# Running the narrow and the wide form of an expert side by side, weight tile by weight tile

## The chip, the cores and the metric

The kernel runs on one NeuronCore of a Trainium2 chip. The metric is the device time of one execution in microseconds. TensorE (PE in the profile; PEld is its weight load) multiplies, VectorE (DVE) and ScalarE (ACT) work elementwise, GpSimd (POOL) does small copies, and SyncE (SP) issues the DMAs that bring the weights from HBM.

## The reference

One encoder layer, 256 tokens of width 2048, float32. A first half (modulated norm, input projection, attention, spatial gating, output projection, norm) is not touched by the change. The second half is a mixture of 32 experts: each token goes to two experts of one group of eight.

```python
    xs = xf[row_tok].reshape(n_blocks, EXPERT_BLOCK, d)      # rows sorted by expert

    def expert_block(args):
        xb, e = args
        hb = jax.nn.silu(xb @ w_gate[e]) * (xb @ w_up[e])    # 2048 -> 512
        return hb @ w_down[e]                                # 512 -> 2048
...
    out = jax.ops.segment_sum(ys * row_w[:, None], row_tok, num_segments=n)
```

So 512 rows (256 tokens, two experts each) are spread over 32 experts as the router has it, and every expert with at least one row needs its 12 MB of float32 weights. The result goes into a last residual and norm.

## The kernel before, in words

**First half** (to about 770 us). Modulation vectors, projections and attention stream their weights through a ring of SBUF tiles. None of it is changed.

**The experts.** The rows of all experts lie side by side, sorted by expert, as columns of `xs`. On the chip the experts are sorted by their number of rows, and the order of work is a list of 32 *places* (`place`, lines 140 to 144): place 0 is expert 0, and of the rest those with the most rows stand at the places 2, 6, 10, 14, 18 and 22 (`WIDE`, line 40). A group is four places, so each of the first six groups has a wide place third. Places 24 to 31 run only if they have rows; in this data 28 places run.

**The weight ring.** A place needs twelve tiles of 1 MB: eight with gate and up weights (`gu`, 256 rows of the contraction each) and four with down weights (`dn`). They go through one ring of 14 tiles (lines 655 and 901: `ring`, `ringw`, `ringm`, `ringl`). SP issues the loads in order (`chunk`, line 92, called by `load_place`); a load into a tile waits until TensorE's last read of the tile's former weights.

**The narrow form** (`narrow`) takes the first 32 rows of the expert. As each gate-up tile arrives, TensorE multiplies it in pieces of 128 columns at four places of the array (shape 128x32, four products at a time, line 955). Then `act`: silu on ACT (934), product on DVE (935), transpose on TensorE (938), copy on ACT (939). The down product (961) again goes tile by tile into `pdn`. DVE multiplies `pdn` by the gate and puts it into 32 rows of `y4` (966). After four places `add_four` spreads `y4` over the tokens by a product with slot weights `sl` and adds it into the residual `xa` (1088, 1089), with squares on ACT (1081) for the last norm.

**The wide form** (`wide`) takes rows 33 to 96 of an expert (`xw`, 64 columns, copied by POOL ahead of the place). In `at_place` a wide place loads its row count into registers of PE, ACT and DVE, runs `narrow` up to its last down product, and then, inside `tc.If(v > 32)` on these three engines, the whole of `wide`: a product that selects the expert's slots and weights (`sel_rows`, 1003), two slot-weight tiles on DVE (917, 918), gate-up over all eight tiles once more (978, shape 128x64, two at a time), the same activation chain, the down product (985), two multiplications on DVE (990), and eight products and additions into `xa` (`add_rows`, 926 and 928). Only then come the narrow form's four multiplications into `y4`.

**The order.** TensorE, ACT and DVE run in program order (`manual_schedule`), as do SP and POOL. `group` runs three places, then makes the group's slot weights (`sel_rows` with a small copy `selt` on DVE, line 1001, then a product and `slot_rows`), then the fourth place, then `add_four`.

Of the kernel before, what the change touches and what calls it, by code (L numbers as in the profile page):

```python
# [11 lines left out]
AF = mybir.ActivationFunctionType  # L12
# [4 lines left out]
KT = 16  # L17
NT = 2
T = 256
# [24 lines left out]
def trunk_kernel(ctx, tc, x, c_t, w_ada1, w_ada2, b_ada, b_adac, w_in, sgu_wt, sgu_b, sgu_ln, w_pr, w_o, w_r, b_r,  # L44
                 w_gu, w_down, ln1_c, ln1_g, ln1_b, ln2_g, ln2_b, out):
    nc = tc.nc
# [19 lines left out]
    def k1(name, dt=F32):  # L66
        return wk.tile([128, 256], dt, name=name, tag="k1", bufs=5)
# [4 lines left out]
    def pb(name):  # L72
        return ps.tile([128, 512], F32, name=name, tag="pb", bufs=4)
# [844 lines left out]
        V.tensor_mul(sl, sl, psl[:, 256:])  # L918
        return sl

    def add_rows(sl, y):

        for n in range(NT):
            for j in range(4):
                po = pb("po")
                TE.matmul(po, sl(j)[:, n * 128:(n + 1) * 128], y(j), start=True, stop=True)
                s = xa[n][:, 512 * j:512 * (j + 1)]
                V.tensor_add(s, s, po)

    def act(p, w, own=None):  # L930

        sg, hb, hbT = [own[:, 256 * i:256 * (i + 1)] for i in range(3)] if own is not None else \
            (k1("sg"), k1("hb"), k1("hbT"))
        S.activation(sg[:, :w], p[:, :w], AF.Silu)  # L934
        V.tensor_mul(hb[:, :w], sg[:, :w], p[:, w:2 * w])  # L935
        pt = pa("ptr")
        for i in range(w // 128):
            TE.transpose(pt[:, i * 128:(i + 1) * 128], hb[:, i * 128:(i + 1) * 128], ident)
        S.copy(hbT[:, :w], pt[:, :w])
        return hbT  # L940

    def gate_up(gu, c, k):
        return gu[c].rearrange("p (k a f) -> p k a f", k=2, a=2)[:, k]

    def narrow(gu, dn, rows, el, order=range(8), before_c=None, between=None):

        pn = pa("pgun")
        for i, c in enumerate(order):
            if before_c:
                before_c(i)  # L950
            for k in range(2):
                kt = 2 * c + k
                w = gate_up(gu, c, k)
                for j in range(4):
                    TE.matmul(pn[32 * j:32 * j + 32, :256].rearrange("p (a f) -> p a f", a=2), rows[:, kt],  # L955
                              w[:, :, 128 * j:128 * (j + 1)], start=i + k == 0, stop=i + k == 8)
        hn = act(pn, 128)
        pdn = pa("pdn")
        for j in range(4):
            for n in range(4):  # L960
                TE.matmul(pdn[32 * n:32 * n + 32, :], hn[:, 32 * j:32 * j + 32], dn[j][:, 512 * n:512 * (n + 1)],  # L961
                          start=j == 0, stop=j == 3)
        if between:
            between()
        for n in range(4):
            V.tensor_mul(y4[32 * el:32 * el + 32, 512 * n:512 * (n + 1)], pdn[32 * n:32 * n + 32, :],  # L966
                         gate2[0][32 * n:32 * n + 32, :])

    def wide(gu, dn, rows, col, own=None):


        psl = rows()
        sl = [slot_rows(psl, col + h, own and own[0][:, 1024 + 256 * h:1280 + 256 * h]) for h in range(2)]
        pw = pa("pguw")
        for kt in range(KT):
            w = gate_up(gu, kt // 2, kt % 2)
            for j in range(2):
                TE.matmul(pw[64 * j:64 * j + 64, :].rearrange("p (a f) -> p a f", a=2), xw[:, kt],
                          w[:, :, 256 * j:256 * (j + 1)], start=kt == 0, stop=kt == KT - 1)
        hw = act(pw, 256, own and own[0])  # L980
        pdw = [pb(f"pdw{b}") for b in range(2)]
        for j in range(4):
            l = hw[:, (j % 2) * 128 + 64 * (j // 2):(j % 2) * 128 + 64 * (j // 2) + 64]
            for n in range(4):
                TE.matmul(pdw[n // 2][64 * (n % 2):64 * (n % 2) + 64, :], l, dn[j][:, 512 * n:512 * (n + 1)],
                          start=j == 0, stop=j == 3)
        ys = []
        for b in range(2):
            y = own[1][:, 512 * b:512 * (b + 1)] if own else k2("yw")
            V.tensor_mul(y, pdw[b], g64[:, b])  # L990
            ys.append(y)
        add_rows(lambda j: sl[j % 2], lambda j: ys[j // 2])

    def sel_rows(c0, c1, rep):
        psl = pb("psl")
        lhs = ident[:32, c0:c1]
        if rep == 128:
            lhs = lhs.to_broadcast([32, 128])
        else:
            t = k1("selt")[:32, :128]  # L1000
            V.tensor_copy(t.rearrange("p (e s) -> p e s", s=rep), lhs[:, :, None].to_broadcast([32, c1 - c0, rep]))
            lhs = t
        TE.matmul(psl, lhs, rwT[:32], start=True, stop=True)
        return psl

# [21 lines left out]
    def leftovers():  # L1027

        r, own = ring, (y4, misc[:, 1024:])
        with tc.For_i(0, NE, 1) as i:  # L1030
            va = nc.values_load(cnt[:1, bass.ds(i + AS, 1)], min_val=0, max_val=2)
            with tc.If(va > 0):
                es = nc.sync.value_load(cnt[:1, bass.ds(i + ES, 1)], min_val=0, max_val=NE - 1)
                for t, src in zip(r, sources(bass.ds(es, 1))):
                    nc.sync.dma_start(t, src.rearrange("a p c -> (a p) c"))
                ev = nc.vector.value_load(cnt[:1, bass.ds(i + ES, 1)], min_val=0, max_val=NE - 1)
                rc = wk.tile([128, 2, NT], F32, name="rc", tag="rc")
                V.tensor_copy(rc, rw[:, :, :, bass.ds(ev, 1)].rearrange("p a n e -> p a (n e)"))

                def rows():  # L1040
                    psl = pb("pslf")
                    for n in range(NT):
                        for a in range(2):
                            TE.transpose(psl[:, a * 256 + n * 128:a * 256 + (n + 1) * 128],
                                         rc[:, a, n:n + 1].to_broadcast([128, 128]), ident)
                    return psl

                def rest(j):
                    off = 32 + 64 * j
                    f = nc.vector.value_load(cnt[:1, bass.ds(i + FS, 1)], min_val=0, max_val=512 - off - 1)  # L1050
                    V.tensor_copy(xw, xs[:, :, bass.ds(f + off, 64)])
                    wide(r[:8], r[8:], rows, 1 + 2 * j, own=own)
# [17 lines left out]
    narrow(*first_weights, xs[:, :, :32], 0, order=range(7, -1, -1), before_c=rows0)  # L1070
    gate2_halves()


# [18 lines left out]
    ENG = (E.PE, E.Activation, E.DVE)  # L1092

    def at_place(i, sl=None):
# [3 lines left out]
        if i not in WIDE:  # L1098
            narrow(gu, dn, xnb[i % 2], i % 4)
            return  # L1100
        f = nc.gpsimd.value_load(cnt[:1, WS + i // 4:WS + i // 4 + 1], min_val=32, max_val=512)
        P.tensor_copy(xw, xs[:, :, bass.ds(f, 64)])
        v = nc.values_load(cnt[:1, CS + i:CS + i + 1], engines=ENG, min_val=0, max_val=T)

        def more_rows():
            with tc.If(v > 32):
                wide(gu, dn, lambda: sel_rows(i, i + 1, 128), 1)

        narrow(gu, dn, xnb[i % 2], i % 4, between=more_rows)

    def group(q):
        for i in range(max(1, 4 * q), 4 * q + 3):
            at_place(i)
        sl = slot_rows(sel_rows(4 * q, 4 * q + 4, 32), 0)
        if q == 6:
            tc.mark_branch_hint_location("rare", hint="LikelyTaken", engines=ENG)
        at_place(4 * q + 3)
        add_four(sl)

    l2 = []  # L1120

# [101 lines left out]
```

## Time and profile before

| | |
|---|---|
| three timed runs | 1681.76 us median (1676.31 to 1685.01) |
| the profiled execution's own time | 1673.7 us |
| its span | 1672.0 us |
| TensorE busy, mean granted clock | 1373.1 us (82%), 0.891 |
| DVE, ACT, POOL busy | 797.8, 386.5, 56.6 us |
| HBM read | 572.38 MB, mean 345 GB/s |

The span is the stretch of the profiled execution that has instructions, 1.7 us shorter than its time. The page gives the busy time of each engine and slices the span in forty; the other views give single waits, instructions in order of time, and busy times by stretch. A TensorE that is busy is not at its peak: its products overlap, and the records run on past the end of streaming. Because the page's chain of waits goes back only to the last branch that all engines share (1655.8 us here), the experts' stretch has to be read from the other views.

### The profile page before, as it was taken

The numbers are of one execution on the slowest core, as the hardware profiler recorded it, in microseconds if no ns is written. First come the engines' busy times: TensorE is split into PE (matmuls) and PEld (weight loads), VectorE is DVE, ScalarE is ACT, GpSimd is POOL, SyncE is SP. The second block draws the span as 40 slices with busy tenths as digits, with TensorE's granted clock in tenths as the row PEclk, the third lists the DMA queues.
The fourth block names the chain that finished last, engine by engine and source line by source line (L and its number), as shares of the span: only waits on it lengthen the run. The fifth ranks groups of instructions, "written<-read, shape, count | busy, mean of one in ns | idle before, by whom it ended". The sixth has DMA issues, their size and how long they took to land. (4 is left out here: it accounts for less than half of the span.)

```text
span 1672.0 us, 24699 instructions
## 1 busy us (share of the span) xinstructions
PE 1373.1 (82%) x10150; PEld 862.1 (52%) x10151; DVE 797.8 (48%) x1099; ACT 386.5 (23%) x519; POOL 56.6 (3%) x76
## 2 busy tenths in 40 slices
PE   4999999999999989967788688688688678767664
PEld 3878989989999987744223123123223223222121
DVE  6777879788877767875123013104104104112104
ACT  2533244663333332333101001001001000101002
POOL 0000000001000100000000000000000000000000
PEclk8999999999999998987889789779879889878677
DMA  8978787478998888884988998988998998999994
GB/s 327 363 294 309 308 299 278 173 257 334 336 340 321 308 331 301 325 327 153 417 363 354 421 393 360 421 351 362 421 397 365 421 398 360 420 418 422 421 421 194
DMA packets 80353, 576.17 MB, mean 345 GB/s; under 512 B 9448, under 2 KB 9448, under 8 KB 10600
## 3 DMA queue, kind: packets, MB, share of 16 engines
q1 hardware_dynamic: 78624, 569.41, 85.7%
q10 hardware_dynamic: 1608, 5.10, 0.8%
q8 instruction: 82, 1.34, 0.3%
q14 instruction: 39, 0.32, 0.0%
HBM read 572.38 MB, written 2.10 MB: 344 GB/s over the span
## 5 line engine op out<-in xcount | busy, mean ns | idle before, releaser
L195 DVE TENSOR_TENSOR wl<-ring,wh 128x2048 fp32r<-128x2048 f32 x95 | 217.6, 2291 | 22.7 <-ACT wh L194 22.6
L194 ACT CAST wh<-ring 128x2048 fp32r<-128x2048 f32 x95 | 180.9, 1906 | 152.1 <-DMA ring<-in_w_in 56.5
L935 DVE TENSOR_TENSOR hb<-sg,pgun 128x128 f32<-128x128 f32 x28 | 8.1, 288 | 336.2 <-ACT sg L934 336.2
L342 DVE SCALAR_TENSOR_TENSOR acc<-ring,csg,acc 128x1024 f32<-128x1024 f32 x120 | 153.6, 1280 | 5.9 <-DMA ring<-in_w_ada 4.3
L966 DVE TENSOR_TENSOR y<-pdn,comp 32x512 f32<-32x512 f32 x112 | 76.9, 687 | 159.2 <-PE pdn L961 157.6
L934 ACT ACTIVATE sg<-pgun 128x128 f32<-128x128 f32 x28 | 7.8, 278 | 576.6 <-PE pgun L955 576.6
L203 PE MATMUL a<-hT,wh 128*128 128x256 f32 x384 | 109.7, 287 | 0.0
L204 PE MATMUL a<-hT,wh 128*128 128x256 f32 x384 | 108.2, 283 | 0.0
L205 PE MATMUL a<-hT,wl 128*128 128x256 f32 x384 | 107.8, 284 | 0.0
L955 PE MATMUL pgun<-ringm,misc 128*32 128x256 f32 x1024 | 85.2, 479 | 26.3 <-DMA ringm<-in_w_gu 26.3
L955 PE MATMUL pgun<-ring,misc 128*32 128x256 f32 x992 | 77.2, 454 | 30.1 <-DMA ring<-in_w_gu 30.1
L955 PE MATMUL pgun<-ringw,misc 128*32 128x256 f32 x960 | 76.0, 461 | 30.1 <-DMA ringw<-in_w_gu 30.0
L205 PE MATMUL gb<-hT,wl 128*128 128x256 f32 x256 | 74.2, 290 | 7.5 <-DVE wl L195 7.5
L203 PEld LDWEIGHTS a<-hT,wh 128*128 128x128 f32 x384 | 73.6, 192 | 6.3 <-issue 3.6
L955 PEld LDWEIGHTS pgun<-ringm,misc 128*32 128x32 f32 x1024 | 34.3, 130 | 80.2 <-DMA ringm<-in_w_gu 46.9
L205 PEld LDWEIGHTS a<-hT,wl 128*128 128x128 f32 x384 | 73.1, 192 | 2.1 <-DVE qT L296 0.8
L205 PE MATMUL ga<-hT,wl 128*128 128x256 f32 x256 | 73.0, 285 | 1.1 <-DVE wl L195 1.1
L204 PEld LDWEIGHTS a<-hT,wh 128*128 128x128 f32 x384 | 73.6, 192 | 0.4 <-issue 0.2
L203 PE MATMUL gb<-hT,wh 128*128 128x256 f32 x256 | 73.5, 287 | 0.0
L204 PE MATMUL gb<-hT,wh 128*128 128x256 f32 x256 | 73.1, 286 | 0.0
L203 PE MATMUL ga<-hT,wh 128*128 128x256 f32 x256 | 72.8, 285 | 0.0
L204 PE MATMUL ga<-hT,wh 128*128 128x256 f32 x256 | 72.4, 283 | 0.0
(404 smaller groups left out, 2589.8 us busy)
## 6 DMA issues: line engine op xcount, KB each, us to landing
ring<-in_w_ada SPq DMA_DIRECT2D x87, 1024.0 KB, 6.1
ring<-in_w_gu SPq DMA_DIRECT2D x66, 1024.0 KB, 18.4
ringw<-in_w_gu SPq DMA_DIRECT2D x64, 1024.0 KB, 16.1
ringm<-in_w_gu SPq DMA_DIRECT2D x64, 1024.0 KB, 19.1
ring<-in_w_in SPq DMA_DIRECT2D x63, 1024.0 KB, 6.4
ringm<-in_w_down SPq DMA_DIRECT2D x32, 1024.0 KB, 18.9
ringw<-in_w_down SPq DMA_DIRECT2D x32, 1024.0 KB, 19.7
ring<-in_w_down SPq DMA_DIRECT2D x32, 1024.0 KB, 19.7
```

The source lines that it names most:

```text
L194: S.copy(wh, w)
L195: V.tensor_sub(wl, w, wh)
L203: TE.matmul(acc, lh, rh, start=first, stop=False)
L204: TE.matmul(acc, lh, rl, start=False, stop=False)
L205: TE.matmul(acc, ll, rh, start=False, stop=last)
L342: V.scalar_tensor_tensor(acc, ws, c, acc, op0=ALU.mult, op1=ALU.add)
L934: S.activation(sg[:, :w], p[:, :w], AF.Silu)
L935: V.tensor_mul(hb[:, :w], sg[:, :w], p[:, w:2 * w])
L955: TE.matmul(pn[32 * j:32 * j + 32, :256].rearrange("p (a f) -> p a f", a=2), rows[:, kt], w[:, :, 128 * j:128 * (j + 1)], start=i + k == 0 ...
L966: V.tensor_mul(y4[32 * el:32 * el + 32, 512 * n:512 * (n + 1)], pdn[32 * n:32 * n + 32, :], gate2[0][32 * n:32 * n + 32, :])
```

## The change

`narrow`, `wide`, `act`, `gate_up` and `add_rows` become one function `expert`, which takes the narrow form, the wide form, or both. At the six wide places it runs both, always: the row count is no longer loaded on PE, ACT and DVE, and the `If` is gone. For each gate-up tile TensorE issues the narrow products and then the wide ones, and for each down tile the same. The two activation chains are issued as silu and product of the narrow form, the same of the wide form, the selection product, then transpose and copy of each. The two slot-weight tiles come after that, and the adds of the wide form and the four multiplications into `y4` at the end, in this order. In `group` the product that selects the group's slots moves from between the third and fourth place into the fourth place, between gate-up and transpose (its copy `selt` stays ahead of the place), and `slot_rows` for it moves behind the fourth place.

```diff
+    def expert(gu, dn, narrow=None, wide=None, order=range(8), before_c=None, in_chain=None, own=None):
...
+        pn = narrow and pa("pgun")
+        pw = wide and pa("pguw")
         for i, c in enumerate(order):
...
+            for k in range(2):
+                if narrow:
+                    gate_up(pn, 4, narrow[0], c, k, i)
+            for k in range(2):
+                if wide:
+                    gate_up(pw, 2, xw, c, k, i)
+        hn = narrow and hidden(pn, 128)
+        hw = wide and hidden(pw, 256)
+        extra = in_chain and in_chain()
+        if wide:
+            psl = wide[0]()
+        hn = narrow and turned(*hn, 128)
+        hw = wide and turned(*hw, 256)
+        if wide:
+            sl = [slot_rows(psl, wide[1] + h, own and own[0][:, 1024 + 256 * h:1280 + 256 * h]) for h in range(2)]
+        pdn = narrow and pa("pdn")
+        pdw = wide and [pb(f"pdw{b}") for b in range(2)]
         for j in range(4):
             for n in range(4):
+                d = dn[j][:, 512 * n:512 * (n + 1)]
+                if narrow:
+                    TE.matmul(pdn[32 * n:32 * n + 32, :], hn[:, 32 * j:32 * j + 32], d, start=j == 0, stop=j == 3)
             for n in range(4):
...
+                if wide:
...
+                    TE.matmul(pdw[n // 2][64 * (n % 2):64 * (n % 2) + 64, :], l, d, start=j == 0, stop=j == 3)
...
-        v = nc.values_load(cnt[:1, CS + i:CS + i + 1], engines=ENG, min_val=0, max_val=T)
-
-        def more_rows():
-            with tc.If(v > 32):
-                wide(gu, dn, lambda: sel_rows(i, i + 1, 128), 1)
-
-        narrow(gu, dn, xnb[i % 2], i % 4, between=more_rows)
+            wide = lambda: sel_rows(ident[:32, i:i + 1].to_broadcast([32, 128])), 1
+        return expert(gu, dn, (xnb[i % 2], i % 4), wide, in_chain=in_chain)
 
     def group(q):
         for i in range(max(1, 4 * q), 4 * q + 3):
             at_place(i)
-        sl = slot_rows(sel_rows(4 * q, 4 * q + 4, 32), 0)
...
-        at_place(4 * q + 3)
-        add_four(sl)
+        t = k1("selt")[:32, :128]
+        V.tensor_copy(t.rearrange("p (e s) -> p e s", s=32), ident[:32, 4 * q:4 * q + 4, None].to_broadcast([32, 4, 32]))
+        psl = at_place(4 * q + 3, lambda: sel_rows(t))
+        add_four(slot_rows(psl, 0))
```

## Rows read from the trace of the kernel before

**Rows 1.** The page: the span, and of the 40 slices of the span (41.8 us each) the granted TensorE clock in tenths and what the DMA engines moved.

```profile
span 1672.0 us, 24699 instructions
...
PEclk8999999999999998987889789779879889878677
...
GB/s 327 363 294 309 308 299 278 173 257 334 336 340 321 308 331 301 325 327 153 417 363 354 421 393 360 421 351 362 421 397 365 421 398 360 420 418 422 421 421 194
```

**Rows 2.** Busy time by stretch from the second expert on: per row the stretch, its length, then busy us and instruction count of PE, PEld, DVE, ACT and POOL, the granted TensorE clock as a share of 2.4 GHz, the DMA share and the GB/s moved. The middle stretch holds all the wide branches that were taken.

```profile
800.00:840.00 40.00, 29.94 (x330) 10.63 (x322) 6.27 (x12) 2.61 (x7) 1.23 (x2) 0.82 1.01 422
840.00:1470.00 630.00, 490.12 (x3785) 169.79 (x3785) 137.75 (x269) 44.53 (x128) 17.02 (x24) 0.86 0.94 387
1470.00:1620.00 150.00, 101.29 (x809) 30.53 (x805) 23.01 (x47) 9.23 (x26) 2.47 (x4) 0.72 1.01 420
```

**Rows 3.** The same view around the first wide place, 840 to 890 us, same columns.

```profile
840.00:842.50 2.50, 1.08 (x12) 0.16 (x8) 0.00 (x0) 0.00 (x0) 0.00 (x0) 0.86 1.01 419
842.50:852.50 10.00, 10.00 (x34) 2.92 (x32) 1.72 (x4) 0.00 (x0) 0.00 (x0) 0.69 0.48 172
852.50:880.00 27.50, 22.85 (x90) 7.82 (x86) 9.64 (x15) 0.76 (x2) 0.00 (x0) 0.99 1.01 422
880.00:887.50 7.50, 6.79 (x62) 2.88 (x66) 1.52 (x4) 0.00 (x0) 0.00 (x0) 0.59 0.24 79
887.50:890.00 2.50, 2.50 (x52) 1.40 (x48) 0.00 (x0) 0.00 (x0) 0.00 (x0) 1.00 1.05 334
```

**Rows 4.** Waits of the SP queue, which issues the weight loads: who waited at which line for whom, us in total, times, longest.

```profile
SPq L92 <- PE pgun L955: 132.4, 69, 14.2
SPq L92 <- PE pguw L978: 124.8, 40, 19.9
```

**Rows 5.** The SP queue's timeline over the first of these gaps: start, us from the first to the last issue, queue, line, tile, count of transfers issued (1024 KB each).

```profile
848.74 2.09 SPq L92 DMA_DIRECT2D ringm<-in_w_gu  x2
852.21 0.33 SPq L92 DMA_DIRECT2D ring<-in_w_gu  x1
```

**Rows 6.** Timeline around the first wide place: start, us, engine, line, operation, tile, shapes, count; in brackets the idle time ahead and what ended it. An fp32 product shows as two records. Narrow gate-up paced by the DMA; selection product; wide gate-up (16, 32 and 16 records); silu; wide down; the first add into the residual rows; the four narrow evictions.

```profile
826.54 1.85 PE L955 MATMUL pgun<-ring,misc 128*32 128x256 f32 x16 [0.63 <-DMA ring<-in_w_gu]
843.01 2.07 PE L1003 MATMUL psl<-rwT,ident 32*128 32x512 f32 x2
845.01 5.44 PE L978 MATMUL pguw<-ringm,xw 128*64 128x512 f32 x16
850.28 7.03 PE L978 MATMUL pguw<-ring,xw 128*64 128x512 f32 x32
857.15 3.60 PE L978 MATMUL pguw<-ringw,xw 128*64 128x512 f32 x16
860.85 0.38 ACT L934 ACTIVATE sg<-pguw 128x256 f32<-128x256 f32 x1 [25.92 <-PE pguw L978]
862.70 3.65 PE L985 MATMUL pdw<-ringw,hbT 128*64 128x512 f32 x16 [0.52 <-ACT hbT L939]
868.98 0.69 DVE L990 TENSOR_TENSOR yw<-pdw,misc 128x512 f32<-128x512 f32 x1 [7.29 <-PE pdw L985]
869.73 7.13 PE L926 MATMUL po<-yw,sl 128*128 128x512 f32 x16
877.61 2.79 DVE L966 TENSOR_TENSOR y<-pdn,comp 32x512 f32<-32x512 f32 x4
```

**Rows 7.** TensorE's timeline in the narrow place after it, where the tiles had landed before TensorE came to them.

```profile
887.89 3.63 PE L955 MATMUL pgun<-ring,misc 128*32 128x256 f32 x64
```

**Rows 8.** TensorE's timeline where one shape of product follows another without a wait: narrow down (128x32), selection (32x128) and wide gate-up (128x64) at 1362 us, granted clock 1.00; selection and narrow gate-up at 1495 us, clock 0.5.

```profile
1362.63 1.06 PE L961 MATMUL pdn<-ringw,hbT 128*32 128x512 f32 x8 [1.43 <-DMA ringw<-in_w_down]
1363.63 1.12 PE L1003 MATMUL psl<-rwT,ident 32*128 32x512 f32 x2
1364.68 3.65 PE L978 MATMUL pguw<-ringl,xw 128*64 128x512 f32 x16
...
1495.48 2.07 PE L1003 MATMUL psl<-rwT,selt 32*128 32x512 f32 x2 [3.16 <-DVE selt L1001]
1497.47 1.94 PE L955 MATMUL pgun<-ringm,misc 128*32 128x256 f32 x16
```

**Rows 9.** By line: the one that turns a selection product into slot weights (two runs for each wide branch taken, one for each group of four), and the wide gate-up's records on one kind of tile. Count, ns min/median/max, first and last start.

```profile
L917 DVE TENSOR_SCALAR sl<-psl,slotc x17: 476/483/486, 845.1 to 1617.9; 128x256 f32<-128x256 f32 x17
L978 PE MATMUL pguw<-ringm,xw x96: 592/592/1116, 845.0 to 1374.6; 128*64 128x512 f32 x96
```

**Rows 10.** Timeline of the last place (27) and the end: slot weights of the last group, the last weight tile, evictions, the products that add the group, the first and the last addition.

```profile
1617.94 0.48 DVE L917 TENSOR_SCALAR sl<-psl,slotc 128x256 f32<-128x256 f32 x1 [1.77 <-PE psl L1003]
1618.45 0.42 DVE L918 TENSOR_TENSOR sl<-sl,psl 128x256 f32<-128x256 f32 x1
1642.40 1.81 PE L961 MATMUL pdn<-ring,hbT 128*32 128x512 f32 x8 [0.55 <-DMA ring<-in_w_down]
1644.29 2.85 DVE L966 TENSOR_TENSOR y<-pdn,comp 32x512 f32<-32x512 f32 x4 [10.61 <-PE pdn L961]
1645.03 7.45 PE L1088 MATMUL po<-y,sl 128*128 128x512 f32 x16 [0.82 <-DVE y L966]
1647.17 0.69 DVE L1089 SCALAR_TENSOR_TENSOR xa<-po,xa 128x512 f32<-128x512 f32 x1
1652.51 0.69 DVE L1089 SCALAR_TENSOR_TENSOR xa<-po,xa 128x512 f32<-128x512 f32 x1 [0.16 <-PE po L1088]
```

More of the change, by code (lines that the diff above doesn't have):

```diff
@@ L919, in slot_rows, with gate_up, hidden, turned @@
         return sl
[L921 to L947, printed above, removed]
+    def expert(gu, dn, narrow=None, wide=None, order=range(8), before_c=None, in_chain=None, own=None):
+        def gate_up(acc, tiles, x, c, k, i):
+            w = gu[c].rearrange("p (k a f) -> p k a f", k=2, a=2)[:, k]
+            m = 128 // tiles
+            f = 512 // tiles
+            for j in range(tiles):
+                TE.matmul(acc[m * j:m * j + m, :2 * f].rearrange("p (a f) -> p a f", a=2), x[:, 2 * c + k],
+                          w[:, :, f * j:f * (j + 1)], start=i + k == 0, stop=i + k == 8)
+        def hidden(acc, w):
+            sg, hb, hbT = [own[0][:, 256 * i:256 * (i + 1)] for i in range(3)] if own else \
+                (k1("sg"), k1("hb"), k1("hbT"))
+            S.activation(sg[:, :w], acc[:, :w], AF.Silu)
+            V.tensor_mul(hb[:, :w], sg[:, :w], acc[:, w:2 * w])
+            return hb, hbT
+        def turned(hb, hbT, w):
+            pt = pa("ptr")
+            for i in range(w // 128):
+                TE.transpose(pt[:, i * 128:(i + 1) * 128], hb[:, i * 128:(i + 1) * 128], ident)
+            S.copy(hbT[:, :w], pt[:, :w])
+            return hbT
+        pn = narrow and pa("pgun")
+        pw = wide and pa("pguw")
         for i, c in enumerate(order):
@@ L951, in narrow @@
             for k in range(2):
[L952 to L958, printed above, removed]
+                if narrow:
[3 more added lines that the diff above has]
+                    gate_up(pw, 2, xw, c, k, i)
@@ L960, in narrow @@
             for n in range(4):
[L961 to L983, printed above, removed]
-            for n in range(4):
[L985 to L992, printed above, removed]
@@ L994, in sel_rows @@
-    def sel_rows(c0, c1, rep):
-        psl = pb("psl")
[L996 to L1002, printed above, removed]
+                d = dn[j][:, 512 * n:512 * (n + 1)]
+                if narrow:
+                    TE.matmul(pdn[32 * n:32 * n + 32, :], hn[:, 32 * j:32 * j + 32], d, start=j == 0, stop=j == 3)
@@ new lines, in expert @@
+            for n in range(4):
+                d = dn[j][:, 512 * n:512 * (n + 1)]
+                if wide:
+                    l = hw[:, (j % 2) * 128 + 64 * (j // 2):(j % 2) * 128 + 64 * (j // 2) + 64]
+                    TE.matmul(pdw[n // 2][64 * (n % 2):64 * (n % 2) + 64, :], l, d, start=j == 0, stop=j == 3)
+        if wide:
+            ys = []
+            for b in range(2):
+                y = own[1][:, 512 * b:512 * (b + 1)] if own else k2("yw")
+                V.tensor_mul(y, pdw[b], g64[:, b])
+                ys.append(y)
+            for n in range(NT):
+                for j in range(4):
+                    po = pb("po")
+                    TE.matmul(po, sl[j % 2][:, n * 128:(n + 1) * 128], ys[j // 2], start=True, stop=True)
+                    s = xa[n][:, 512 * j:512 * (j + 1)]
+                    V.tensor_add(s, s, po)
@@ L1003, in sel_rows @@
+        if narrow:
+            el = narrow[1]
+            for n in range(4):
+                V.tensor_mul(y4[32 * el:32 * el + 32, 512 * n:512 * (n + 1)], pdn[32 * n:32 * n + 32, :],
+                             gate2[0][32 * n:32 * n + 32, :])
+        return extra
+    def sel_rows(lhs):
+        psl = pb("psl")
         TE.matmul(psl, lhs, rwT[:32], start=True, stop=True)
@@ L1051, in rest @@
                     V.tensor_copy(xw, xs[:, :, bass.ds(f + off, 64)])
-                    wide(r[:8], r[8:], rows, 1 + 2 * j, own=own)
+                    expert(r[:8], r[8:], None, (rows, 1 + 2 * j), own=own)
                 vl = nc.values_load(cnt[:1, bass.ds(i + LS, 1)], min_val=0, max_val=1)
@@ L1068, in leftovers @@
                 squares(n, b, s, pb("sq"))
-    narrow(*first_weights, xs[:, :, :32], 0, order=range(7, -1, -1), before_c=rows0)
+    expert(*first_weights, (xs[:, :, :32], 0), order=range(7, -1, -1), before_c=rows0)
     gate2_halves()
@@ L1090, in add_four, with at_place @@
                 squares(n, b, s, po)
-    ENG = (E.PE, E.Activation, E.DVE)
-    def at_place(i, sl=None):
+    def at_place(i, in_chain=None):
         gu, dn = load_place(i)
@@ L1097, in at_place @@
         P.tensor_copy(xnb[i % 2], xs[:, :, bass.ds(f, 32)])
[L1098 to L1102, printed above, removed]
-        v = nc.values_load(cnt[:1, CS + i:CS + i + 1], engines=ENG, min_val=0, max_val=T)
-        def more_rows():
-            with tc.If(v > 32):
-                wide(gu, dn, lambda: sel_rows(i, i + 1, 128), 1)
-        narrow(gu, dn, xnb[i % 2], i % 4, between=more_rows)
+        wide = None
+        if i in WIDE:
+            f = nc.gpsimd.value_load(cnt[:1, WS + i // 4:WS + i // 4 + 1], min_val=32, max_val=512)
+            P.tensor_copy(xw, xs[:, :, bass.ds(f, 64)])
+            wide = lambda: sel_rows(ident[:32, i:i + 1].to_broadcast([32, 128])), 1
+        return expert(gu, dn, (xnb[i % 2], i % 4), wide, in_chain=in_chain)
     def group(q):
@@ L1113, in group @@
             at_place(i)
-        sl = slot_rows(sel_rows(4 * q, 4 * q + 4, 32), 0)
         if q == 6:
-            tc.mark_branch_hint_location("rare", hint="LikelyTaken", engines=ENG)
-        at_place(4 * q + 3)
-        add_four(sl)
+            tc.mark_branch_hint_location("rare", hint="LikelyTaken", engines=(E.PE, E.Activation, E.DVE))
+        t = k1("selt")[:32, :128]
+        V.tensor_copy(t.rearrange("p (e s) -> p e s", s=32), ident[:32, 4 * q:4 * q + 4, None].to_broadcast([32, 4, 32]))
+        psl = at_place(4 * q + 3, lambda: sel_rows(t))
+        add_four(slot_rows(psl, 0))
     l2 = []
```

## The prediction

> **What bounds the kernel now.** First the page's slices: from slice 20 on, where the experts run, the DMA engines move 417 to 422 GB/s in ten slices and 351 to 398 in a repeating pattern in ten others, while the granted clock shows digits of 6 to 9 [rows 1]. So the weights' stream is the bound there, and something interrupts it. By stretch: 422 GB/s from 800 to 840 us, 387 from 840 to 1470, 420 from 1470 to 1620 [rows 2]. At 421 GB/s a 1 MB tile (1.0486 MB) takes 2.49 us and a place of twelve 29.9 us. The missing part of the middle stretch is 630 x (1 - 387/421) = 50.9 us (49.5 with 420, 52.2 with 422).
>
> The wide branch is what interrupts it. Line 917 runs twice for each branch taken and once for each of seven groups, 17 times in all: five of the six wide places took it [rows 9]; the first starts at 845 us and place 22 did not take it. Around the first one the stream has two gaps: 10 us at 172 GB/s, which lose 10 x (1 - 172/421) = 5.9 us, and 7.5 us at 79 with 2.5 us at 334, which lose 6.1 + 0.5 = 6.6 us; between them it runs at 422 with TensorE busy for 22.9 of 27.5 us [rows 3]. The reason is the ring: the twelve tiles of a wide place are read a second time after the narrow form is through, so at 845 us none of them is free, and SP waits for line 978 for 124.8 us in all [rows 4]. It issues again at 848.74, when TensorE has been through the first tiles [rows 5]. The second gap begins when the wide form's adds, the four evictions (877.61 to 880.4) and the group's selection product stand between the branch and the next place's first product [rows 6].
>
> **The change part by part.** *Gate-up and down side by side.* At full clock a narrow tile costs TensorE 0.86 us: 64 records (four tiles) take 3.63 us, of which some 0.2 is the last record's tail [rows 7]. A wide tile costs 1.71 us: 32 records, four tiles, in 7.03 less 0.2 [rows 6]. A down tile streams the same columns in the same shapes and costs the same: 8 narrow records in 1.06 less 0.2 [rows 8], 16 wide ones (two tiles) in 3.65 [rows 6]. Together 2.57 us, a little above the 2.49 at which tiles land. New are the changes of shape, two per tile. Three rows show such a change without a wait: from narrow down to selection 1363.63 - 1362.63 less 0.86 of streaming = 0.14 us, from selection to wide gate-up 1.05 - 0.86 = 0.19, from selection to narrow gate-up at half clock 1.99 - 1.72 = 0.27 [rows 8]. I take 0.2; bounds 0 (columns stream no faster for a change of shape, so no gain) and 0.27. A tile then costs 2.97 us (2.57 to 3.11).
>
> The Trainium skill, TensorEngine Tiling (Array Packing), Key Properties, says that changing the tiling mode drains TensorE, which speaks against exactly this interleaving; it has no price. These rows agree that a change costs something, and small; what 24 of them in a row cost no run here shows.
>
> How far does TensorE fall behind the stream in one wide place? Twelve tiles at 2.97 are 35.6 us. The first wide gate-up began at clock 0.5 and took 5.27 us for 16 records that take 3.43 at full clock, so 1.8 us for a start at 1.2 GHz [rows 6]. Silu to first down product 860.85 to 862.70, 1.9 us, already has TensorE idle for silu and product, and the moved selection product, 1.05 us at full clock [rows 8], stands in that idle time. From the first multiplication to the end of the adds, 868.98 to 876.86, of which some 0.6 lies beside the last down records: 7.3 us [rows 6]. Sum 46.6 against 29.9: 16.7 us behind, with the 1.9 us of a narrow tile at half clock [rows 6] ahead of it 18.6 us, or 7.5 tiles. The ring has 14. Six are left for the stream, and after the first gap it was back at full rate with three issued (two from 848.74, one at 852.21) [rows 3, 5]. So the stream starves only from 11 tiles or 27.4 us behind, and does not. The next narrow place catches up: 0.86 against 2.49 us per tile. I therefore count the whole 50.9 us as gained.
>
> *The branch at place 22.* It now runs its wide form, some 30 us more of TensorE's work. The cover is the same: the place ends 18.6 us behind, inside the ring. Without that cover it would cost what the others lose now, 50.9/5 = 10.2 us.
>
> *Register loads and branches gone; slot weights and `xw`.* Nothing waits on them once the stream is the bound. The two slot-weight tiles (four DVE operations, 1.8 us by their kind in rows 10) lie beside the down products. No load is added: POOL and SP issue what they issued, in the same order.
>
> *The group's selection product.* It leaves the head of TensorE's queue before the fourth place, where it waited for `selt` behind the evictions (3.16 us idle, 2.07 us of work at 1495 us) [rows 8]. Between 1470 and 1620 us this already cost the stream nothing [rows 2], so I count no gain; the wide places' second gap holds its part elsewhere. In its new place it stands beside silu and product.
>
> *The end of the last group.* Here nothing covers. The last tile's products end at 1644.21 and the evictions at 1647.14; the slot weights were ready since 1618.9, so the group's products began at 1645.03 and the first add at 1647.17 [rows 10]. After the change the two slot-weight operations (0.48 + 0.42 us) stand behind the evictions, and the first product starts at about 1648.1, after 3.9 us without work on TensorE. After a like idle time the selection product ran at 1.2 GHz, two records in 2.07 us [rows 8]. With three pairs at that clock (2.07 + 2 x 1.72) and five at 0.86, the last add starts at 1657.9 instead of 1652.51: 5.4 us later. Bounds: 0.9 if the products were off the path, 9.7 if all eight ran at half clock.
>
> **Sum.** 1673.7 (the profiled execution's own time) - 50.9 + 5.4 = 1628.2. The median of the runs shown stands 8.1 us above that execution, and I carry this over: 1636.
>
> **Rivals.** *The second gap stays.* If TensorE is more than 27.4 us behind at the end of a wide place, the stream still stops there, now in six places. Saved is then the first gap's share, 50.9 x 5.9/12.5 = 24.0; place 22 adds 10.2 x 6.6/12.5 = 5.4, the end 5.4: 1673.7 - 13.2 + 8.1 = 1669. For it: the second gap is the larger one, and the adds stay behind the down products. Against: 8.8 us are missing to that point.
>
> *Slower: changes of shape.* If each costs much more in this alternation than in rows 8, TensorE is the bound of a wide place. Break-even is where six places lose 45.5 us, 7.6 each, 35 us behind; that is 16.4/12 = 1.37 us more per tile, 4.34 us, or 0.88 us per change. At 1.1 us per change, as long as the slowest wide record lasted [rows 9], a tile costs 4.77 us, a place falls 18.6 + 12 x 1.8 = 40.2 us behind and loses 12.8: 1628.2 + 6 x 12.8 + 8.1 = 1713. Against: the rows show 0.14 to 0.27 [rows 8].
>
> *The stream doesn't run on.* The gaps close, but 421 GB/s isn't held with TensorE busy throughout: at a mean of 392 over the middle stretch the gain is 630 x (1 - 387/392) = 8.0 us less the 5.4 of the end: 1679, no change. Against: 422 in the stretch where TensorE was busy most [rows 3].
>
> **How the numbers follow.** Forecast 0.82, second gap 0.10, slower 0.05, stream 0.03. The forecast's own range: 52.2 gained and 0.9 lost from the lowest run shown (1676.3) is 1625, 49.5 and 9.7 from the highest (1685.0) is 1645. Ten per cent beyond would reach the second gap's 1669; a part of it (two or three places) is about 1655. I give 1620 to 1658. A measurement of this kernel can tell about 0.5%, 8 us. Of the second gap 0.08 counts as faster and 0.02 as the same; with the stream's case 0.90 faster, 0.05 same, 0.05 slower.
>
> **What would show it.** Right: from 840 us to the last load 415 GB/s or more in every slice, no 10 us stretch under 350; six pairs of wide slot weights; line-92 waits of SP for TensorE mostly gone in favour of waits for DMA; in wide places 2.6 to 3.1 us per tile at granted clock 1.00; the last load 50 us earlier, the end 45 us earlier; in the last group the slot weights behind the evictions. Wrong: gaps in the stream at the fourth place of each group (second gap), wide tiles above 3.9 us (changes of shape), or a stream of under 410 GB/s without gaps.

## The result and the profile after

The kernel after takes 1632.9 us (median of 4 runs, 1632.6 to 1636.2) against 1679.0 (4 runs, 1676.3 to 1685.0): ratio 0.9725, 95% interval 0.9692 to 0.9758. Its profiled execution took 1632.55 us, span 1630.9. The prediction was 1636 us, range 1620 to 1658.

The page of the kernel after, the lines that answer to [rows 1]: span, busy times, granted clock in tenths and GB/s of 40 slices (40.8 us each).

```profile
span 1630.9 us, 24878 instructions
PE 1382.5 (85%) x10266; PEld 862.0 (53%) x10267; DVE 808.5 (50%) x1114; ACT 388.9 (24%) x521; POOL 56.6 (3%) x76
...
PEclk9899999999999998996999699799699799798777
...
GB/s 323 356 255 315 335 275 302 178 246 310 347 321 338 318 309 333 309 340 163 342 421 420 422 421 420 422 421 420 421 420 421 421 421 421 421 420 421 421 421 123
```

From slice 21 to slice 39 every slice moves 420 to 422 GB/s; the pattern of 351 to 398 is gone. TensorE is busy 9 us more in all, with one wide place more. The same by stretch, answering to [rows 2], columns as there:

```profile
800.00:840.00 40.00, 38.92 (x386) 13.83 (x379) 6.27 (x12) 5.31 (x12) 1.24 (x2) 0.96 1.01 422
840.00:1470.00 630.00, 524.46 (x4105) 175.16 (x4105) 151.66 (x291) 47.88 (x134) 18.09 (x26) 0.87 1.01 421
1470.00:1600.00 130.00, 85.27 (x696) 26.26 (x695) 20.05 (x42) 8.95 (x25) 1.36 (x3) 0.76 0.99 410
```

421 GB/s in the middle stretch, where 387 stood; in the last one the loads end. SP's waits between 800 and 1640 us, answering to [rows 4] (there over the whole span):

```profile
SPq L92 <- DMA ringm<-in_w_gu: 101.5, 62, 2.0
...
SPq L92 <- PE pgun L930: 7.0, 15, 1.7
...
SPq L92 <- PE pguw L930: 1.3, 5, 0.3
```

SP, at line 92, waits for TensorE's gate-up products (now line 930) at most 1.7 us at a time, 7.0 and 1.3 us in all; nearly all of its waiting there is for transfers under way. Line 917 ran 19 times, two for each of six wide places and one for each of seven groups [rows 9]:

```profile
L917 DVE TENSOR_SCALAR sl<-psl,slotc x19: 477/484/485, 841.0 to 1601.7; 128x256 f32<-128x256 f32 x19
```

The first wide place of the kernel after, TensorE's timeline (start, us, line, tile, shapes, count), with the first tiles of the place behind it:

```profile
831.23 1.07 PE L930 MATMUL pgun<-ring,misc 128*32 128x256 f32 x16
832.23 1.94 PE L930 MATMUL pguw<-ring,xw 128*64 128x512 f32 x8
834.10 1.07 PE L930 MATMUL pgun<-ringw,misc 128*32 128x256 f32 x16
...
839.84 1.12 PE L1001 MATMUL psl<-rwT,ident 32*128 32x512 f32 x2
...
841.62 1.07 PE L973 MATMUL pdn<-ringw,hbT 128*32 128x512 f32 x8 [0.19 <-ACT hbT L944]
...
853.08 7.13 PE L988 MATMUL po<-yw,sl 128*128 128x512 f32 x16
...
860.15 3.66 PE L930 MATMUL pgun<-ringm,misc 128*32 128x256 f32 x64
...
871.67 1.06 PE L973 MATMUL pdn<-ringw,hbT 128*32 128x512 f32 x8 [0.82 <-DMA ringw<-in_w_down]
```

A tile (narrow from 831.23, wide, next narrow at 834.10) takes 2.87 us. The selection product stands between gate-up and transpose, the down product starts 1.9 us after gate-up ends, the adds end at 860.2 and the next place starts at once, at 860.15. The last row is that place's eleventh tile, on which TensorE waited: it landed at 871.67, so at 2.49 us per tile the first had landed at 846.8. TensorE was 13.4 us, 5.4 tiles, behind the stream when it came to it. Worked out in the same way, it was 12.3 to 15.6 us behind at the other five wide places; the three highest, 14.2 to 15.6, are those that began at half clock (1.2 GHz).

Where did the time go? The first half of the kernel differs by some us from one execution to the next (the first expert product starts at 771.12 us in the profile before, at 774.14 in the one after), so the table counts from the first expert product to the start of the last down tile, and from there to the last addition into the residual. The column of gaps sums, over stretches of 2.5 us from 800 us on under 400 GB/s and before the loads end, what was missing to 421 GB/s; its last digit is rough.

| profile | first product to last down tile | gaps | last down tile to last addition |
|---|---|---|---|
| before | 871.3 | 51.5 | 10.1 |
| after | 823.6 | 0 | 13.7 |
| e1_serial | 838.4 | 18.1 | 15.4 |
| e2_move | 849.7 | 28.7 | 14.3 |
| e3_slots | 823.7 | 0 | 10.0 |
| e4_nowide | 823.6 | 0 | 16.1 |
| e5_twice8 | 827.1 | 6.7 | 13.9 |
| e6_thrice8 | 901.8 | 81.4 | 13.8 |
| e7_switch | 823.7 | 0 | 15.2 |
| e8_nobranch | 884.6 | 65.4 | 10.7 |
| e11_move_nobranch | 851.6 | 31.3 | 13.6 |

So the change won 47.7 us in the stream, gave back 3.5 at the end, and its profiled execution started the experts 3.0 us later: 1673.7 - 47.7 + 3.5 + 3.0 = 1632.5.

One caution on the rows of kernels with gaps. Each row is one execution, and the gap at the start of a wide form (the first gap) comes in two sizes, by the granted clock at which TensorE begins the wide gate-up (loss per gap worked out as in the column of gaps):

| profile | first gaps begun at full clock, us | begun at half clock, us |
|---|---|---|
| before | 2.9, 2.4, 2.3 | 5.9, 7.1 |
| e2_move | 2.9 | 6.6, 6.3, 6.0, 6.6 |
| e8_nobranch | 2.9, 3.8, 3.3 | 6.0, 5.9, 6.6 |
| e11_move_nobranch | 3.4, 2.5 | 6.0, 6.5, 6.9, 6.1 |
| e1_serial | 2.8, 2.4, 1.6 | 3.8, 4.1, 3.4 |

The two kinds in the trace before are the place at 845 us, where 16 wide records took 5.27 us [rows 6], and the one at 1364.68 us [rows 8], where they took 3.48 us and the stream lost 2.3 us:

```profile
1365.00:1367.50 2.50, 2.50 (x14) 0.86 (x12) 1.51 (x4) 0.00 (x0) 0.00 (x0) 1.00 0.43 177
1367.50:1370.00 2.50, 2.50 (x14) 0.84 (x12) 0.00 (x0) 0.00 (x0) 0.00 (x0) 1.00 0.87 275
```

A TensorE at half clock takes longer to free the first tiles. How many places of a kernel begin so differs from trace to trace, two of five before and four of five in e2_move, so a difference of some us between two rows with gaps can come from that alone. Whether an edit itself has a part in it is not shown.

### The profile page after: what moved, and what is told of

The parts are those of the page before. It is cut to its first block, busy times and chain, and to the rows that moved or that the text cites. A ratio compares the mean times of both kernels' runs of the same rounds, so it can differ in the third digit from the quotient of the medians.

```text
span 1630.9 us, 24878 instructions
## 1 busy us (share of the span) xinstructions
PE 1382.5 (85%) x10266; PEld 862.0 (53%) x10267; DVE 808.5 (50%) x1114; ACT 388.9 (24%) x521; POOL 56.6 (3%) x76
## 5 line engine op out<-in xcount | busy, mean ns | idle before, releaser
L930 PE MATMUL pgun<-ringm,misc 128*32 128x256 f32 x1024 | 76.1, 437 | 17.6 <-DMA ringm<-in_w_gu 17.6
L1086 PE MATMUL po<-y,sl 128*128 128x512 f32 x112 | 64.2, 738 | 27.2 <-DVE sl L918 27.2
L930 PE MATMUL pgun<-ringw,misc 128*32 128x256 f32 x960 | 72.5, 441 | 16.8 <-DMA ringw<-in_w_gu 16.8
L930 PE MATMUL pgun<-ring,misc 128*32 128x256 f32 x992 | 69.9, 421 | 13.7 <-DMA ring<-in_w_gu 13.6
```

The source lines that it names most:

```text
L930: TE.matmul(acc[m * j:m * j + m, :2 * f].rearrange("p (a f) -> p a f", a=2), x[:, 2 * c + k], w[:, :, f * j:f * (j + 1)], start=i + k == 0 ...
L1086: TE.matmul(po, sl[:, n * 128:(n + 1) * 128], y4[:, 512 * b:512 * (b + 1)], start=True, stop=True)
```

## The experiments

Two theories stood against mine (the stream has two gaps, each closed by another edit): that all of it is the interleaving, and that it is the branch that went. Each kernel's times stand beside runs of the kernel before on the same chip.

**e1_serial**: the interleaving undone.

```diff
-        return expert(gu, dn, (xnb[i % 2], i % 4), wide, in_chain=in_chain)
+        extra = expert(gu, dn, (xnb[i % 2], i % 4), None, in_chain=in_chain)
+        if wide:
+            expert(gu, dn, None, wide)
+        return extra
```

> The kernel after, but at the wide places the two forms run one after the other, still without a condition; the group's selection product stays where the change put it. Theory (the gain is the two gaps in the weight stream, closed by two different edits): the first gap comes back in all six wide places because their twelve tiles are held for a second reading, the second gap stays closed: 4 to 5 us lost per place, 1655 to 1663 us, stream under 300 GB/s for some 10 us once per group, early in the wide part only. Rival A (all of the gain is the interleaving): both gaps back in six places, 1633 + 6 x 10.2 = 1694. Rival B (all of it is the branch and the register loads that went): 1633.

Measured: 1643.2 us (4 runs, 1640.6 to 1647.0), ratio 0.9798 (0.9755 to 0.9841). TensorE's timeline at the first wide place, and the busy times of two stretches with the GB/s last:

```profile
840.48 1.07 PE L973 MATMUL pdn<-ringl,hbT 128*32 128x512 f32 x8 [1.42 <-DMA ringl<-in_w_down]
841.48 3.65 PE L930 MATMUL pguw<-ringm,xw 128*64 128x512 f32 x16
```

```profile
840.00:850.00 10.00, 9.52 (x48) 3.08 (x50) 2.75 (x4) 0.00 (x0) 0.00 (x0) 1.00 0.87 301
850.00:860.00 10.00, 9.54 (x44) 3.05 (x42) 2.14 (x5) 0.76 (x2) 0.00 (x0) 1.00 1.00 420
```

The gap at the start of the wide form is back, once per wide place and nowhere else, so its place is as expected. Its size is not: 18.1 us in six, 3.0 each rather than 4 to 5, and in the stream 14.8 us more than the kernel after; the time, too, lies below the 1655 to 1663 expected. The wide products follow the narrow ones at once, here at full clock (841.48, 16 records in 3.5 us to the next group), where the kernel before had the selection product (2.0 us) in front and began at 1.2 GHz [rows 6]. Three of the six places began at half clock here too and lost 3.4 to 4.1 us.

**e2_move**: in the kernel before, only the group's selection product moved.

```diff
...
-        sl = slot_rows(sel_rows(4 * q, 4 * q + 4, 32), 0)
...
-        at_place(4 * q + 3)
-        add_four(sl)
+        t = k1("selt")[:32, :128]
+        V.tensor_copy(t.rearrange("p (e s) -> p e s", s=32), ident[:32, 4 * q:4 * q + 4, None].to_broadcast([32, 4, 32]))
...
+        at_place(4 * q + 3, sel)
+        add_four(slot_rows(got[0], 0))
```

> The kernel before, with the move of the group's selection product (into the fourth place, slot weights behind it) as the only edit; branch and serial wide form stay. Theory: the gap after the wide place goes (5.4 of the 10.2 us lost in each of five places), the one at its start stays, and the last group ends 3.5 us later as in the trace after: 1679 - 27 + 3.5 = 1655. Rival A: nothing but the later end, 1682. Rival B: the same 1682.

Measured: 1645.0 us (5 runs, 1643.7 to 1655.2), ratio 0.9812 (0.9773 to 0.9852); the profiled execution was the slowest, 1655.2, and the median lies 10 us below the 1655 expected. The first wide place and the place behind it:

```profile
841.68 2.07 PE L1005 MATMUL psl<-rwT,ident 32*128 32x512 f32 x2
843.68 5.42 PE L980 MATMUL pguw<-ringm,xw 128*64 128x512 f32 x16
...
868.37 7.13 PE L926 MATMUL po<-yw,sl 128*128 128x512 f32 x16
875.43 3.66 PE L957 MATMUL pgun<-ringm,misc 128*32 128x256 f32 x64
```

```profile
840.00:850.00 10.00, 9.90 (x32) 2.71 (x34) 1.72 (x4) 0.00 (x0) 0.00 (x0) 0.66 0.50 177
...
880.00:890.00 10.00, 7.50 (x83) 2.66 (x75) 2.29 (x4) 0.55 (x2) 0.62 (x1) 1.00 1.01 418
```

In the kernel before, the group's selection product stood there, and TensorE was idle for 3.85 us until `selt` was made behind the evictions:

```profile
880.71 2.07 PE L1003 MATMUL psl<-rwT,selt 32*128 32x512 f32 x2 [3.85 <-DVE selt L1001]
882.70 5.36 PE L955 MATMUL pgun<-ringm,misc 128*32 128x256 f32 x64
```

With the move the next place's first product starts at 875.43, when the adds of the wide place end. In the kernel before it started at 882.70, 5.8 us after its adds had ended (876.86 [rows 6]). The stretch in which that kernel had its second gap (79 GB/s from 880 us, [rows 3]) moves 418. All five second gaps are gone; in the trace before they come to 30.4 us of the 51.5. The stream is only 871.3 - 849.7 = 21.6 us shorter mainly because four of five first gaps were of the large kind in this execution (28.4 us for the five, 20.6 before). The other four runs were 8.5 to 11.5 us faster, and the median is 30.7 us below that of the kernel before, but only the slowest run has a trace. So the move wins 21.6 us of the change's 47.7 in this trace, and probably more in the other runs. The first gap stays (177 GB/s).

**e8_nobranch**: in the kernel before, only the condition gone. **e11_move_nobranch**: the same with the move.

```diff
-        v = nc.values_load(cnt[:1, CS + i:CS + i + 1], engines=ENG, min_val=0, max_val=T)
...
-            with tc.If(v > 32):
-                wide(gu, dn, lambda: sel_rows(i, i + 1, 128), 1)
+            wide(gu, dn, lambda: sel_rows(i, i + 1, 128), 1)
```

> The kernel before with the condition taken away as the only edit: the register loads and the branch go, the wide form runs serially in all six wide places, the group's selection product stays ahead of the fourth place. Theory: place 22 gets the two gaps of the others (10.2 us) and each wide form starts up to 1.4 us earlier: 1676 + 10 - 5 = 1681, stream gaps in six places. Rival (branch and register loads are what costs): well under 1670.

> The kernel before with two edits: the move of the group's selection product, and the condition taken away (the wide form stays serial, its selection product stays ahead of its gate-up, the narrow evictions stay behind it). It tells which part of e1_serial's lead over e2_move (838.4 against 849.7 us from the first expert product to the last down tile) came from the branch. Theory (a shorter way from the narrow down product to the first freed tile is what counts, and the branch is only 1.4 us of it): the first gap in six places, 4 to 6 us each, 845 to 855 us for that stretch and about 1645 in all. Rival (the branch was the cause of that lead): 838 us and 1640 in all.

Measured: e8_nobranch 1683.6 us (10 runs, 1677.6 to 1692.0), ratio 1.0051 (1.0026 to 1.0076); e11_move_nobranch 1653.7 us (4 runs, 1650.2 to 1660.9), ratio 0.9855 (0.9816 to 0.9893). The branch is not it: without it the kernel before is slower, by place 22's two gaps, 3.3 and 5.9 us, and some more (three first gaps of the large kind rather than two). Where both run at full clock, the selection product starts 1.00 us after the last narrow down products begin with the branch (before, 973.92 to 974.92 us) and 0.99 without it (e8, 838.07 to 839.06). With the move, the stretch is 851.6 us against e2_move's 849.7, although place 22 now has a gap of 6.1 us; that is in the 845 to 855 expected, while the whole time lies 9 us above the 1645. e11's second wide place on TensorE:

```profile
967.87 1.66 PE L963 MATMUL pdn<-ring,hbT 128*32 128x512 f32 x8 [1.43 <-DMA ring<-in_w_down]
969.46 2.07 PE L1005 MATMUL psl<-rwT,ident 32*128 32x512 f32 x2
971.47 4.12 PE L980 MATMUL pguw<-ringw,xw 128*64 128x512 f32 x10
```

The wide gate-up starts 3.6 us after the last narrow down product began, of which 2.0 are the selection product at half clock and no branch is left. So e1_serial's lead of 13.2 us over e11 lies in what else differs: there the selection product comes after the gate-up, and the narrow evictions ahead of the wide form. At like clock e1's first gaps are smaller by some 0.7 us (full) and 2.6 us (half), near the selection product's 1.05 and 2.0 us, and it had three half-clock places to e11's four. No run separated the two orders.

In one chain from before to after, the stream goes 21.6 us down with the move (e2), 1.9 up without the condition (e11, with place 22 added), 13.2 down with the new order in the wide place (e1) and 14.8 down with the interleaving (after), 47.7 in all. Each of these four numbers holds the chance of the clock in the gaps of its kernels.

**e4_nowide**: no wide form at all.

```diff
-WIDE = range(2, 26, 4)
+WIDE = ()
```

> The kernel after without any wide form (the rows 33 to 96 of the six largest experts are left out). Theory (the weight stream is the bound and all of the wide work is covered): the same time, 1631 to 1634. Rival (a part of the wide work, such as the adds, still delays the stream): six times 1 us or more, below 1627.

Measured: 1631.2 us (4 runs, 1629.0 to 1635.1), ratio 0.9733 (0.9692 to 0.9775). The stretch is 823.6 us, as with all six wide forms: in the kernel after they cost the stream nothing.

**e5_twice8** and **e6_thrice8**: how much more TensorE work a wide place takes. `again` (its definition is not shown) is the wide gate-up product into a tile that nobody reads; e6 has it twice.

```diff
...
+        px = wide and not own and pb("pguw2")
...
                     gate_up(pw, 2, xw, c, k, i)
+                    if px is not None and px is not False and i < 8:
+                        again(px, c, k, i)
```

> The kernel after, with every wide gate-up product run a second time into a PSUM tile that nobody reads: 8 tiles x 1.71 us = 13.7 us more of TensorE in each wide place. Theory (a 14-tile ring lets TensorE fall some 27 us behind before the stream stops; the trace after shows it 13.4 us behind at the end of the first wide place): 27.1 us behind, just at the edge, 0 to 2 us lost per place, 1633 to 1645 us, no stretch of 10 us under 300 GB/s. Rival (any further work on TensorE in the wide places is paid): 6 x 13.7 = 82 us more, 1715.

> The same with the wide gate-up products run three times, 27.4 us more in each wide place. Theory: 40.8 us behind, 13 us over the edge in each of six places: 1633 + 6 x 13.4 = 1713 us, with gaps in the stream in and after each wide place. Rival (all is paid): 1633 + 164 = 1797. Rival (TensorE's work in the wide places does not matter at all): 1633.

Measured: 1634.8 us (4 runs, 1632.1 to 1638.3), ratio 0.9759 (0.9725 to 0.9792), and 1709.5 us (4 runs, 1706.9 to 1710.0), ratio 1.0209 (1.0180 to 1.0239). 13.7 us more per place cost 3.5 us in the whole stream; 27.4 us more cost 901.8 - 823.6 = 78.2 us, 13.0 per place where 13.4 was worked out. The second wide place of e6_thrice8, and the stretch behind it up to the next:

```profile
990.00:1022.50 32.50, 32.31 (x217) 11.16 (x217) 12.27 (x21) 1.20 (x4) 0.61 (x1) 1.00 0.67 247
1022.50:1110.00 87.50, 73.49 (x609) 26.24 (x603) 15.60 (x33) 8.14 (x22) 2.91 (x4) 0.90 1.01 421
```

32.5 us at 247 GB/s lose 32.5 x (1 - 247/421) = 13.4 us with TensorE busy throughout at granted clock 1.00; then the stream runs full. The edge of some 27 us behind lies between these two doses, close to the first: in e5_twice8 the places that begin at full clock lost 0 and 0.3 us, the four whose first tile ran at half clock, wholly or in part, 1.2 to 2.1.

**e7_switch**: four changes of shape per gate-up tile.

```diff
             for k in range(2):
                 if narrow:
                     gate_up(pn, 4, narrow[0], c, k, i)
-            for k in range(2):
                 if wide:
                     gate_up(pw, 2, xw, c, k, i)
```

> The kernel after, with narrow and wide products alternating after each 128 rows of the contraction and so four changes of shape per gate-up tile rather than two. Theory: each change costs about 0.15 us (2.87 us per tile in the trace after less 2.57 of streaming, halved), so a tile takes 3.17 us, a wide place falls 2.4 us further behind, and the time stays 1631 to 1635. Rival (changes of shape drain for much longer when they come closer): tiles over 3.5 us.

Measured: 1631.6 us (4 runs, 1629.7 to 1635.2), ratio 0.9739 (0.9710 to 0.9769), the stretch 823.7 us. TensorE's timeline:

```profile
822.76 0.64 PE L930 MATMUL pgun<-ringm,misc 128*32 128x256 f32 x8
823.33 1.08 PE L930 MATMUL pguw<-ringm,xw 128*64 128x512 f32 x4
824.34 0.64 PE L930 MATMUL pgun<-ring,misc 128*32 128x256 f32 x8
824.91 1.08 PE L930 MATMUL pguw<-ring,xw 128*64 128x512 f32 x4
825.92 0.64 PE L930 MATMUL pgun<-ring,misc 128*32 128x256 f32 x8
```

From 822.76 to 825.92 it is 3.16 us for one tile's worth with four changes. With 2.57 of streaming that is 0.15 us for each, as with two (2.87). The changes stay cheap, and hidden.

**e3_slots, e10_slots**: slot weights of the group inside the fourth place's chain; e10 is the same kernel again, run side by side with the kernel after (e9_after).

```diff
-        psl = at_place(4 * q + 3, lambda: sel_rows(t))
-        add_four(slot_rows(psl, 0))
+        sl = at_place(4 * q + 3, lambda: slot_rows(sel_rows(t), 0))
+        add_four(sl)
```

> The kernel after, with the group's slot weights made on VectorE right behind the selection product, inside the fourth place's chain, rather than behind its evictions. Theory: the end is the only place where that order is on the path, and the 3.5 us that the last group's end grew by come back: 1629.4, with the first addition about 2.9 us after the evictions begin, as in the kernel before. Rival: VectorE's queue now waits for the selection product ahead of the evictions and nothing is gained, 1633.

> The kernel after once more, as the other side of the next run on the same chip: 1628 to 1636.

> The version with the group's slot weights made inside the fourth place's chain, with more rounds and beside the kernel after. Theory: 3.5 us (0.2%) less than the kernel after in the same call, from the last group's end alone. Rival: no difference beyond the spread of single runs.

Measured: e3_slots 1628.1 us (4 runs, 1624.5 to 1630.0), ratio 0.9714 (0.9674 to 0.9753). Side by side, e9_after 1631.9 us (6 runs, 1631.3 to 1632.5), ratio 0.9734 (0.9703 to 0.9765), and e10_slots 1625.9 us (6 runs, 1624.4 to 1634.4), ratio 0.9709 (0.9673 to 0.9744). The end of e3_slots, DVE and TensorE:

```profile
1584.07 0.48 DVE L917 TENSOR_SCALAR sl<-psl,slotc 128x256 f32<-128x256 f32 x1 [0.36 <-PE psl L1001]
...
1593.15 1.69 PE L973 MATMUL pdn<-ring,hbT 128*32 128x512 f32 x8 [0.52 <-DMA ring<-in_w_down]
1594.91 2.85 DVE L994 TENSOR_TENSOR y<-pdn,comp 32x512 f32<-32x512 f32 x4 [9.90 <-PE pdn L973]
1595.65 7.45 PE L1086 MATMUL po<-y,sl 128*128 128x512 f32 x16 [0.81 <-DVE y L994]
1597.79 0.69 DVE L1087 SCALAR_TENSOR_TENSOR xa<-po,xa 128x512 f32<-128x512 f32 x1
...
1603.13 0.69 DVE L1087 SCALAR_TENSOR_TENSOR xa<-po,xa 128x512 f32<-128x512 f32 x1 [0.16 <-PE po L1086]
```

The slot weights are made at 1584, the first addition follows the start of the evictions by 2.9 us and the last one the last down tile by 10.0, as in the kernel before [rows 10]. The medians of e9 and e10 are 6.0 us apart, more than the 3.5 expected. One of e10's six runs is slower than all of e9's and the ratios' intervals overlap, so the gain is read from the traces (last down tile to last addition: 15.9 us in e9_after, 10.2 in e10_slots); it has the lowest medians run here.

## Why the prediction was right, point by point

*The bound and its gaps*: right. The stream of weights runs at 421 GB/s without a gap, and 823.6 us is what it needs, the same without any wide work (e4_nowide).

*50.9 us gained*: 47.7 measured from the first expert product to the last down tile. The term was the missing share of one stretch against 421 GB/s; with the 420 that the kernel after holds from 843 us to the end of the loads it would have been 49.5. The remaining 1.8 us are about what half a GB/s in each of the two rounded rates makes (0.8 and 0.9 us).

*Two gaps, two reasons*: right in place. But the prediction booked both in one term and wrote of the group's selection product that it counts no gain for the move. As an account of what each edit does that step was wrong: the move alone closes all five second gaps and is worth 21.6 us in the stream of its trace (e2_move). Nor did it see that the first gap has two sizes, 2.3 to 2.9 us at full clock and 5.9 to 7.1 at half in the trace before; it worked out only the first, at half clock. What the rows between 1470 and 1620 us showed, that the product costs the stream nothing there, holds only where TensorE is not already behind.

*2.97 us per tile with 0.2 per change of shape*: 2.87, with 0.15. The Trainium skill, TensorEngine Tiling (Array Packing), Key Properties, has a change of tiling mode drain TensorE; the trace agrees that it costs time, 0.15 us each at 2.4 GHz, with two (2.87 us) and with four (3.16 us) changes per tile.

*18.6 us behind, edge at 27.4*: 13.4 at the first wide place, since it began at full clock and the tiles were cheaper, and at most 15.6 where the first tile ran at half clock. The edge held: 13.7 us more (e5) cost 3.5 us in all, 27.4 us more (e6) cost 13.0 per place. That three transfers under way keep the stream full was read from one gap; the two doses bear out the sum, not that number by itself.

*Branch and register loads at nothing*: right (e8, e11; the selection product starts no sooner without them).

*Place 22 at nothing*: right; the whole wide work is hidden (e4).

*The end 5.4 us later*: right in kind. The kernel after, end of the last group:

```profile
1597.71 1.07 PE L973 MATMUL pdn<-ring,hbT 128*32 128x512 f32 x8 [1.29 <-DMA ring<-in_w_down]
1598.85 2.80 DVE L994 TENSOR_TENSOR y<-pdn,comp 32x512 f32<-32x512 f32 x4 [9.25 <-PE pdn L973]
1601.66 0.48 DVE L917 TENSOR_SCALAR sl<-psl,slotc 128x256 f32<-128x256 f32 x1
...
1602.66 8.67 PE L1086 MATMUL po<-y,sl 128*128 128x512 f32 x16 [3.88 <-DVE sl L918]
1604.77 0.69 DVE L1087 SCALAR_TENSOR_TENSOR xa<-po,xa 128x512 f32<-128x512 f32 x1 [2.17 <-PE po L1086]
...
1606.21 0.69 DVE L1087 SCALAR_TENSOR_TENSOR xa<-po,xa 128x512 f32<-128x512 f32 x1 [0.74 <-PE po L1086]
...
1607.07 0.69 DVE L1087 SCALAR_TENSOR_TENSOR xa<-po,xa 128x512 f32<-128x512 f32 x1 [0.16 <-PE po L1086]
...
1611.36 0.69 DVE L1087 SCALAR_TENSOR_TENSOR xa<-po,xa 128x512 f32<-128x512 f32 x1 [0.16 <-PE po L1086]
```

The slot weights stand behind the evictions, the first product waits for them, and the first two additions are 1.44 us apart, then 0.86: the granted clock was 0.50 from 1602.66 us to the first addition, 0.65 up to the second and 1.00 behind it. From the last down tile to the last addition it is 13.65 us against 10.11: 3.5, and 5.8 in e9_after's profile (15.9). The prediction's three pairs at half clock are about what e9_after shows (additions 1.71, 1.71 and 1.24 us apart, then 0.86); the kernel after's own profile had about one and a half.

*The sum*: the prediction made 1628.2 for the profiled execution, which took 1632.55: 3.2 less won in the stream, 1.9 less lost at the end, and a first half 3.0 us later, which no term had. The 8.1 us carried over from the median before did not come: the median after stands 0.3 us above its profiled execution. That 1636 lies only 3 us from 1632.9 is in part luck: the one error was 4.3 us too low, the other 7.8 too high. All runs of the kernel before lie from 1670.3 to 1688.1 us, all of the kernel after from 1631.3 to 1636.2; that the two sizes of the first gap made the wider spread is likely, but the other runs have no trace.

*The rivals*: the second gap's did not occur (no stretch under 400 GB/s before the loads end), the dear changes of shape neither, and the stream does run at 421 GB/s with TensorE busy.

## What to carry to other kernels

When a stage is bound by a stream through a ring, ask of every engine only how far it falls behind, in tiles, against what the ring leaves: work below that edge is free, as 13.7 us per place nearly were, and above it each us is paid, as the next 13.7 nearly were in full (12.5). Read a stream's gaps one by one, name the reader that held the ring at each, and note the clock it ran at (the first gap of the kernel before cost 2.3 to 2.9 us at full clock, 5.9 to 7.1 at half); here two small orders of issue (a product ahead of a queue that must wait, and a second pass over tiles already read) each made one. Where a stream hides everything, the end of the last stage is the place to look for what is left: there 0.9 us on VectorE became 3.5 to 5.8.

## What the runs showed of the hardware that was not expected

Behind a gap the stream can run faster than its steady 421 GB/s for a few us. Kernel before, two steps of 2.5 us after its first gap:

```profile
862.50:865.00 2.50, 2.30 (x12) 0.87 (x14) 0.00 (x0) 0.15 (x1) 0.00 (x0) 1.00 1.03 436
865.00:867.50 2.50, 2.50 (x16) 0.78 (x14) 0.00 (x0) 0.00 (x0) 0.00 (x0) 1.00 1.04 436
```

Over the whole trace the effect is small: the eight steps behind a gap average 422.7 GB/s, all other steps outside gaps 420.7, and single steps reach 439 in e4_nowide, which has no gap. A gap's cost worked out from 421 leaves it out.
